# Adaptive units of a down step emitted in two parts, and the gathering matmul of a finished vector three units later

## The chip, the core and the metric

One core of one Trainium2 chip runs the program. The metric is the device time of one execution in microseconds; the time before is the median of three runs. TensorE (PE in the profile; its weight loads are PEld) multiplies matrices into PSUM, VectorE (DVE) and ScalarE (ACT) work element by element, GpSimd (POOL) does a little, and SyncE (SP) issues most of the loads. Each engine runs its own queue of instructions in order and waits on semaphores of the others.

## The reference: what is computed

Two trunk layers over 512 latent tokens of width 1024. Layer 0 mixes with neighbourhood attention and HGRN2 heads (with 256 context tokens), layer 1 with a short gated convolution; each layer ends in a gated feed-forward part of width 2816. Six adaptive vectors per layer (shift, scale and gate of both halves) come from the conditioning vector `c`:

```
mod = silu_c @ ada_w[layer] + ada_b[layer]
shift_m, scale_m, gate_m, shift_f, scale_f, gate_f = jnp.split(mod, 6, axis=-1)
...
x = x + gate_m[:, None, :] * y
h = modulate(rms_norm(x, norm_ffn_w[layer]), shift_f, scale_f)
x = x + gate_f[:, None, :] * conv_ffn(h, ffn_w_up[layer], ffn_conv_w[layer],
                                      ffn_conv_b[layer], ffn_w_down[layer])
...
def conv_ffn(h, w_up, conv_w, conv_b, w_down):
    a, val = jnp.split(h @ w_up, 2, axis=-1)
    return (jax.nn.gelu(dwconv3(a, conv_w, conv_b), approximate=False) * val) @ w_down
```

`ada_w` is 1024 by 6144 for each layer, 25 MB, and is used for one row vector only.

## The kernel before

Activations lie transposed: channels on the 128 partitions, tokens along the free dimension. Each matrix product is made of three matmuls (`mm3`, L287 to L290): weights and activations are split into a high and a low half, and high×high, high×low and low×high are added in PSUM. `Weights` loads raw weights with SyncE into two buffers `wraw` (1 MB a load as a rule), makes the high half `whi` with a copy on ScalarE (L92) and the low half `wlo` with a subtraction on VectorE (L93); three buffers of each kind go round, so a copy waits until TensorE has left the oldest.

**The adaptive vectors** that are not needed at once are made on VectorE in the background by `Ada`, in 160 units. A unit loads a slice `ar` of `ada_w` (128 by 512, 256 KB; three buffers, loaded by SyncE two units ahead, L485) and adds slice times conditioning into the accumulator `aa` (L502 for the first of eight slices, L504 for the others). After eight units a transposing reduction (L508) gives `ad`; this ends one half of a vector. A later unit, counted in calls, issues `gather`, a matmul on TensorE of `ad` with a selecting matrix into the PSUM tile `pad` (L514), and a still later one `finish`, four small additions on VectorE into `mod` (L520) and for the scales one more (L524). 20 such halves are made, the first of layer 0's mixer aside.

**Where units are issued.** 54 units are woven into layer 0's mixer. Then `units(n)` issues them in blocks: four in layer 0's output projection, five in each of eleven steps of layer 0's down projection, three at a time in layer 1's convolution mixer, four in each of two steps of its output projection, and two after groups of its feed-forward up part.

**The steps of the down projection** are in `project_back`. It makes 256 output channels at a time (four pairs `m`) and for each pair three groups of 6, 8 and 8 of the 22 input blocks. A step takes two weight tiles, then issues five units, then the matmuls of the first output tile `o[0]` (8 blocks by 3 matmuls of 512 columns is 24), then those of `o[1]`. The order of the built program need not be the order of the code: a scheduler places each instruction in its engine's queue by its own estimate of when its inputs are there, except where `pin` holds the order of the code.

Of the kernel before, what the change touches and what calls it, by code (L numbers as in the profile page):

```python
# [174 lines left out]
def backbone(ctx: ExitStack, tc: tile.TileContext, a, out, dump=None):  # L175
# [107 lines left out]
    def split(hi, lo, src):  # L283
        S.copy(hi, src)
        V.tensor_tensor(lo, src, hi.bitcast(F32), ALU.subtract)

    def mm3(o, wh, wl, mh, ml, start, stop):  # L287
        TE.matmul(o, wh, mh, start=start, stop=False, skip_group_check=True)  # L288
        TE.matmul(o, wh, ml, start=False, stop=False, skip_group_check=True)  # L289
        TE.matmul(o, wl, mh, start=False, stop=stop, skip_group_check=True)  # L290
# [183 lines left out]
    class Ada:  # L474
# [3 lines left out]
        n, calls, raw, late = 0, 0, {}, []  # L478
# [9 lines left out]
        def unit(self, aux):  # L488
            self.calls += 1
            while self.late and self.late[0][0] <= self.calls:  # L490
                self.late.pop(0)[1]()
            if self.n >= 8 * len(self.jobs):
                return
            r = self.n % 8
            l, p_, j = self.jobs[self.n // 8]
            while len(self.raw) < min(self.n + 3, 8 * len(self.jobs)):
                self.load()
            raw = self.raw[self.n]
            self.n += 1
            if r == 0:  # L500
                self.acc = ap_.tile([P, T], F32, tag="aacc", name=f"aa{self.n}", bufs=1)
                pin(V.tensor_scalar(self.acc[:], raw[:], sil[:, 0, 0:1], None, ALU.mult))  # L502
                return
            pin(V.scalar_tensor_tensor(self.acc[:], raw[:], sil[:, r, 0:1], self.acc[:], ALU.mult, ALU.add))  # L504
            if r < 7:
                return
            red = ap_.tile([P, 16], F32, tag="ared", name=f"ad{self.n}", bufs=1)
            V.tensor_reduce(red[:], self.acc[:].rearrange("p (b j) -> p b j", j=32), axis=AX.X, op=ALU.add,  # L508
                            apply_transpose=True)
            pm = []  # L510

            def gather():
                pm.append(aux(f"pad{l}{p_}{j}"))
                TE.matmul(pm[0][:, 0:16], sel, red[:], start=True, stop=True)  # L514

            def finish():
                c = p_ * 8 + 4 * j
                for qd in range(4):
                    s4 = slice(32 * qd, 32 * qd + 32)
                    V.tensor_tensor(mod[s4, l, c : c + 4], pm[0][s4, qd:16:4], abT[s4, l * 48 + c : l * 48 + c + 4],  # L520
                                    ALU.add)
                if p_ in (1, 4):
                    w0 = (16 if p_ == 1 else 32) + 8 * l + 4 * j
                    V.scalar_tensor_tensor(amul[:, 2 * l + (1 if p_ == 1 else 2), 4 * j : 4 * j + 4], mod[:, l, c : c + 4],  # L524
                                           1.0, pv[:, w0 : w0 + 4], ALU.add, ALU.mult)

            self.late += [(self.calls + 3, gather), (self.calls + 5, finish)]

    ada = Ada()

# [450 lines left out]
    def mms(o, w, src, base, k0, k1, c, first, last):  # L981
        wh, wl = w
        for k in range(k0, k1):
            hh, hl = src[k]
            mm3(o[:, c], wh[:, k - base], wl[:, k - base], hh[:, c], hl[:, c], first and k == base, last and k == k1 - 1)
# [49 lines left out]
    def project_back(nm, src, groups, gate, norm, start=0):  # L1035


        A, B = HALF
        steps = [(m, g_) for m in range(start, 4) for g_ in range(len(groups))]

        for n, (mp_, gi) in enumerate(steps):
            k0, k1 = groups[gi]
            if gi == 0:
                o = [acc_t(f"pb{nm}{mp_}{i}") for i in range(2)]
            w = [ws.get(), ws.get()]
            first, lastg = gi == 0, gi == len(groups) - 1
            if n == len(steps) - 1:
                break
            if n == len(steps) - 2:
                ws.spare = [(gq, f"q{2 * i}", f"q{2 * i + 1}") for i in range(3)]  # L1050
                ws.ahead(4)
            if n < len(steps) - 2 or len(groups) > 1:
                units(4 if len(groups) == 1 else 5)
            for i in range(2):
                mms(o[i], w[i], src, k0, k0, k1, slice(0, T), first, lastg)
                if lastg:
                    norm.back(o[i], 2 * mp_ + i, slice(0, T), gate)
                    if mp_ or i:
                        norm.add(slice(0, T))

        cut = (k0 + 3 * k1) // 4
        ws.ahead(4)
        mms(o[0], w[0], src, k0, k0, k1, A, first, True)
        norm.back(o[0], 6, A, gate)
        norm.add(A)
        log_exp_table()
        mms(o[1], w[1], src, k0, k0, k1, A, first, True)
        norm.back(o[1], 7, A, gate)
        norm.add(A)
        mms(o[0], w[0], src, k0, k0, cut, B, False, False)  # L1070
        norm.total(A)
        norm.scale(A)
        mms(o[0], w[0], src, k0, cut, k1, B, False, True)
        mms(o[1], w[1], src, k0, k0, k1, B, False, True)
        norm.back(o[0], 6, B, gate)
        oa = norm.outs(A)
        for _ in range(4):
            next(oa)
        norm.add(B)
        norm.back(o[1], 7, B, gate)  # L1080
        next(oa)
        next(oa)
        norm.add(B)
        for _ in oa:
            pass

        def rest():
            norm.total(B)
            norm.scale(B)
            for _ in norm.outs(B):  # L1090
                pass

        return rest

    def pair(nm, src):

        w = [ws.get(), ws.get()]
        o = [acc_t(f"pp{nm}{i}") for i in range(2)]
        for i in range(2):
            mms(o[i], w[i], src, 0, 0, KT, slice(0, T), True, True)  # L1100
        return o

    def quad(nm, src, rest, done=lambda: None):

        w = [ws.get(0) for _ in range(4)]
        o = [acc_t(f"pp{nm}{i}") for i in range(4)]
        for c in HALF:
            for k in range(KT):
                for i in range(4):
                    hh, hl = src[k]  # L1110
                    mm3(o[i][:, c], w[i][0][:, k], w[i][1][:, k], hh[:, c], hl[:, c], k == 0 and c.start == 0,
                        k == KT - 1)
                if c.start == 0 and k == 3:
                    rest()
        done()
        ws.pin = pin
        ws.ahead(2)
        ws.pin = lambda i: i
        return o[:2], o[2:]
# [91 lines left out]
    def conv3(t, src, w0, w1, w2, b):  # L1211
        S.activation(t[:], src, AF.Identity, scale=w1, bias=b)
        V.scalar_tensor_tensor(t[:, 1:], src[:, : T - 1], w0, t[:, 1:], ALU.mult, ALU.add)
        V.scalar_tensor_tensor(t[:, : T - 1], src[:, 1:], w2, t[:, : T - 1], ALU.mult, ALU.add)
# [8 lines left out]
    def units(n):  # L1223
        for _ in range(n):
            ada.unit(aux_t)
# [52 lines left out]
    for j in range(4):  # L1278
        if j == 0:
            oc, ou = quad("c", nrm.h, rest)  # L1280
        else:
            oc = pair(f"c{j}", nrm.h)
            units(3)
        cs = []
        for i in range(2):
            t = gp.tile([P, T], F32, tag=f"g{16 + i}", name=f"cs{j}{i}")
            S.copy(t[:], oc[i][:])
            cs.append(t)
        if j:
            ou = pair(f"u{j}", nrm.h)  # L1290
            units(3)
        ts_ = []
        for i in range(2):
            m = 2 * j + i
            V.tensor_tensor(cs[i][:], ou[i][:], cs[i][:], ALU.mult)
            t = fp.tile([P, T], F32, tag="t", name=f"sc{m}", bufs=5)
            conv3(t, cs[i], rowv(76 + m, 1), rowv(84 + m, 1), rowv(92 + m, 1), rowv(68 + m, 1))
            ts_.append(t)
        ob = pair(f"b{j}", nrm.h)
        units(3)  # L1300
        for i in range(2):
            m = 2 * j + i
            mh = gp.tile([P, T], F32R, tag=f"g{2 * m}", name=f"mch{m}")
            ml = gp.tile([P, T], F32R, tag=f"g{2 * m + 1}", name=f"mcl{m}")
            V.tensor_tensor(ob[i][:], ob[i][:], ts_[i][:], ALU.mult)
            split(mh[:], ml[:], ob[i][:])
            mix.append((mh, ml))
# [120 lines left out]
```

## Time and profile before

| | |
|---|---|
| median of 3 runs (lowest, highest) | 1335.97 us (1333.49, 1336.93) |
| the profiled execution's own time | 1333.99 us |
| its span in the trace | 1332.2 us |
| busy: TensorE, VectorE, ScalarE | 1304.5, 965.4, 625.2 us |
| mean granted clock of TensorE | 0.995 |

The span is the stretch from the first to the last instruction; the time holds 1.8 us more around it. A matmul's end is modelled, and matmuls overlap, so spacing is read from the starts. An engine's idle time is put down to what released it. Times in the trace count from the span's start.

### The profile page before, as it was taken

What the parts mean: (1) busy time and instruction counts of PE and PEld (TensorE: products, weight loads), DVE (VectorE), ACT (ScalarE), POOL (GpSimd) and SP (SyncE); (2) the same over time, 40 slices, a digit from 0 to 9 for tenths busy, and PEclk for the clock granted to TensorE, in tenths of its full rate; (3) what the DMA queues carried; (4) which work ended last, traced back from release to release, by engine and by line L of the source; (5) the groups of instructions that cost most, each with busy time, mean ns of one, the idle gap of its engine ahead of it and who ended that gap; (6) DMA issues with size and microseconds to landing.
All of it is one profiled execution on the core that took longest, in us unless ns stands there. A gap on an engine that the chain in (4) does not pass through costs nothing. (4 is left out here: it accounts for less than half of the span.)

```text
span 1332.2 us, 21229 instructions
## 1 busy us (share of the span) xinstructions
PE 1304.5 (98%) x8456; PEld 1147.6 (86%) x8456; DVE 965.4 (72%) x1688; ACT 625.2 (47%) x1085; POOL 84.3 (6%) x87
## 2 busy tenths in 40 slices
PE   7999999999999999999999999999999999999997
PEld 4798888888779998889877898888999989899997
DVE  4668897887778878788766776667789897782333
ACT  4443445555545656565422253223456565663223
POOL 2204332311000000000000000000000000000000
PEclk9999999999999999999999999999999999999999
DMA  9842113674562122323466734555403423242231
GB/s 293 265 123 84 33 33 82 152 182 134 153 206 96 64 99 92 127 71 119 141 211 198 226 132 143 167 165 174 158 27 117 142 80 127 80 146 69 91 108 64
DMA packets 134995, 172.35 MB, mean 129 GB/s; under 512 B 14320, under 2 KB 103792, under 8 KB 129776
## 3 DMA queue, kind: packets, MB, share of 16 engines
q1 hardware_dynamic: 132896, 166.15, 39.3%
q10 hardware_dynamic: 2000, 4.85, 1.4%
q8 instruction: 66, 1.08, 0.3%
q14 instruction: 33, 0.27, 0.1%
HBM read 165.21 MB, written 2.10 MB: 126 GB/s over the span
## 5 line engine op out<-in xcount | busy, mean ns | idle before, releaser
L92 ACT CAST whi<-wraw 128x1024 fp32r<-128x1024 f32 (+1 forms) x122 | 124.1, 1021 | 280.8 <-PE pd L1340 70.4
L93 DVE TENSOR_TENSOR wlo<-wraw,whi 128x1024 fp32r<-128x1024 f32 (+1 forms) x122 | 145.2, 1192 | 107.7 <-ACT whi L92 107.1
L288 PE MATMUL p<-hf,whi 128*128 128x512 f32 (+1 forms) x640 | 215.4, 338 | 1.4 <-ACT whi L125 1.4
L290 PE MATMUL p<-hf,wlo 128*128 128x512 f32 (+1 forms) x640 | 214.6, 335 | 0.0
L289 PE MATMUL p<-hf,whi 128*128 128x512 f32 (+1 forms) x640 | 214.1, 335 | 0.0
L125 ACT CAST whi<-wraw 128x512 fp32r<-128x512 f32 (+1 forms) x160 | 113.0, 727 | 85.0 <-PE p L289 35.0
L290 PEld LDWEIGHTS p<-hf,wlo 128*128 128x128 f32 x640 | 120.1, 188 | 13.6
L288 PEld LDWEIGHTS p<-hf,whi 128*128 128x128 f32 x640 | 120.1, 188 | 12.3 <-ACT whi L125 1.6
L289 PEld LDWEIGHTS p<-hf,whi 128*128 128x128 f32 x640 | 120.1, 188 | 10.7
L126 DVE TENSOR_TENSOR wlo<-wraw,whi 128x512 fp32r<-128x512 f32 (+1 forms) x160 | 128.1, 817 | 0.9 <-ACT whi L125 0.5
L504 DVE SCALAR_TENSOR_TENSOR aa<-ar,sil,aa 128x512 f32<-128x512 f32 x140 | 104.8, 749 | 24.1 <-DMA ar<-in_ada_w_dram 21.8
L1339 PE MATMUL pd<-whi,g 128*128 128x256 f32 x352 | 98.2, 279 | 0.0
L1341 PE MATMUL pd<-wlo,g 128*128 128x256 f32 x352 | 98.1, 279 | 0.0
L1340 PE MATMUL pd<-whi,g 128*128 128x256 f32 x352 | 97.9, 278 | 0.0
L288 PE MATMUL pbd<-g,whi 128*128 128x512 f32 (+1 forms) x192 | 73.5, 383 | 0.0
L289 PE MATMUL pbd<-g,whi 128*128 128x512 f32 (+1 forms) x192 | 73.3, 382 | 0.0
L290 PE MATMUL pbd<-g,wlo 128*128 128x512 f32 (+1 forms) x192 | 73.1, 381 | 0.0
L288 PE MATMUL p<-T,whi 128*128 128x256 f32 x240 | 69.0, 288 | 0.0
L290 PE MATMUL p<-T,wlo 128*128 128x256 f32 x240 | 67.2, 280 | 0.0
L289 PE MATMUL p<-T,whi 128*128 128x256 f32 x240 | 67.2, 280 | 0.0
L1340 PEld LDWEIGHTS pd<-whi,g 128*128 128x128 f32 x352 | 66.3, 188 | 0.0
L1339 PEld LDWEIGHTS pd<-whi,g 128*128 128x128 f32 x352 | 66.1, 188 | 0.0
(679 smaller groups left out, 3296.3 us busy)
## 6 DMA issues: line engine op xcount, KB each, us to landing
ar<-in_ada_w_dram SPq DMA_DIRECT2D x160, 256.0 KB, 3.1
wraw<-in_upq_dram SPq DMA_DIRECT2D x40, 1024.0 KB, 4.8
wraw<-in_ffn_w_down_dram SPq DMA_DIRECT2D x16, 1024.0 KB, 5.3
wraw<-in_od_w_in_dram SPq DMA_DIRECT2D x12, 1024.0 KB, 5.6
wraw<-in_ev_w_in_dram SPq DMA_DIRECT2D x20, 512.0 KB, 5.2
araw<-in_ada_w_dram SPq DMA_DIRECT2D x16, 512.0 KB, 6.3
wraw<-in_ffn_w_down_dram SPq DMA_DIRECT2D x8, 768.0 KB, 4.7
wraw<-in_ev_w_out_dram SPq DMA_DIRECT2D x4, 1024.0 KB, 6.9
```

The lines of the kernel that those rows point to most:

```text
L92: self.nc.scalar.copy(hv, rv)
L93: self.pin(self.nc.vector.tensor_tensor(lv, rv, hv.bitcast(F32), ALU.subtract))
L125: self.nc.scalar.copy(hi, src)
L126: V.tensor_tensor(lo, src, hi.bitcast(F32), ALU.subtract)
L288: TE.matmul(o, wh, mh, start=start, stop=False, skip_group_check=True)
L289: TE.matmul(o, wh, ml, start=False, stop=False, skip_group_check=True)
L290: TE.matmul(o, wl, mh, start=False, stop=stop, skip_group_check=True)
L504: pin(V.scalar_tensor_tensor(self.acc[:], raw[:], sil[:, r, 0:1], self.acc[:], ALU.mult, ALU.add))
L1339: TE.matmul(o[i][:, 0:256], gh[:, ts], w[0][:, k - k0], start=k == 0, stop=False)
L1340: TE.matmul(o[i][:, 0:256], gl[:, ts], w[0][:, k - k0], start=False, stop=False)
L1341: TE.matmul(o[i][:, 0:256], gh[:, ts], w[1][:, k - k0], start=False, stop=k == FT - 1)
```

## The change

Two numbers and two places are changed. The gather of a finished vector half is issued six calls after its last unit instead of three, and its finish eight instead of five. In `project_back` the units of a step are issued in two parts: two ahead of the first output tile's matmuls, and the rest (three in the down steps, two in the steps with one group) between the two tiles. The third block of each convolution step issues four units instead of three. The units, loads, reductions, gathers and finishes are the same in number; lines behind the second place move by two.

```diff
-            self.late += [(self.calls + 3, gather), (self.calls + 5, finish)]
+            self.late += [(self.calls + 6, gather), (self.calls + 8, finish)]
...
             if n < len(steps) - 2 or len(groups) > 1:
-                units(4 if len(groups) == 1 else 5)
+                units(2)
             for i in range(2):
                 mms(o[i], w[i], src, k0, k0, k1, slice(0, T), first, lastg)
+                if i == 0 and (n < len(steps) - 2 or len(groups) > 1):
+                    units(2 if len(groups) == 1 else 3)
                 if lastg:
                     norm.back(o[i], 2 * mp_ + i, slice(0, T), gate)
...
         ob = pair(f"b{j}", nrm.h)
-        units(3)
+        units(4)
```

The first piece is TensorE's queue in the second step of the down projection, before: `pbd000` and `pbd001` are the step's two output tiles, `whi` and `wlo` the halves of their weights, `g` the activations, and `pad051` the gather of the half `ad64`. First the last matmuls of the first tile, and then:

```order
L288 MATMUL pbd000_6919<-g0130_6051,whi130_6867 128x512
L289 MATMUL pbd000_6919<-g0131_6052,whi130_6867 128x512
L290 MATMUL pbd000_6919<-g0130_6051,wlo130_6868 128x512
L514 MATMUL pad051_7000<-ad64_6991,cst_70 128x16
L288 MATMUL pbd001_6920<-g060_5347,whi131_6978 128x512
L289 MATMUL pbd001_6920<-g061_5348,whi131_6978 128x512
```

In the changed program the same gather stands behind the second tile's 24 matmuls, ahead of the third step's first:

```order
L288 MATMUL pbd001_6920<-g0130_6051,whi131_6974 128x512
L289 MATMUL pbd001_6920<-g0131_6052,whi131_6974 128x512
L290 MATMUL pbd001_6920<-g0130_6051,wlo131_6975 128x512
L514 MATMUL pad051_7067<-ad64_6991,cst_70 128x16
L288 MATMUL pbd000_6919<-g0140_6199,whi132_6980 128x512
L289 MATMUL pbd000_6919<-g0141_6200,whi132_6980 128x512
```

It has moved by 24 matmuls. The gather `pad101` of the half `ad80` moves likewise, from row 3754 of TensorE's queue, where 20 matmuls of the fifth step stand ahead of it, to row 3806, behind the first tile of the sixth step: by 52. The last of the six, of `ad104`, moves from row 3984 to row 4001.

The second piece is VectorE's queue from the reduction of that first half on, before: `wlo_7057` is a low half of weights, and the row with `pad` the four additions that finish the vector.

```order
L508 TENSOR_REDUCE ad_6991<-aa_4176 128x16
L502 TENSOR_SCALAR aa_6995<-ar_6939,sil 128x512
L520 TENSOR_TENSOR mod<-pad_7000,vec 32x4 x4
L93 TENSOR_TENSOR wlo_7057<-wraw_6865,whi_7056 128x1024
L504 SCALAR_TENSOR_TENSOR aa_6995<-ar_6988,sil,aa_6995 128x512
```

And in the changed program:

```order
L508 TENSOR_REDUCE ad_6991<-aa_4200 128x16
L502 TENSOR_SCALAR aa_6995<-ar_6953,sil 128x512
L93 TENSOR_TENSOR wlo_7055<-wraw_6865,whi_7054 128x1024
L504 SCALAR_TENSOR_TENSOR aa_6995<-ar_6988,sil,aa_6995 128x512
L504 SCALAR_TENSOR_TENSOR aa_6995<-ar_6993,sil,aa_6995 128x512
L504 SCALAR_TENSOR_TENSOR aa_6995<-ar_7021,sil,aa_6995 128x512
L520 TENSOR_TENSOR mod<-pad_7067,vec 32x4 x4
```

The four additions have moved behind one subtraction and three multiply-adds.

## Rows read from the trace of the kernel before

**Rows 1.** The page: span, TensorE's busy time, and VectorE's multiply-adds of the units.
```profile
span 1332.2 us, 21229 instructions
...
PE 1304.5 (98%) x8456; PEld 1147.6 (86%) x8456; DVE 965.4 (72%) x1688; ACT 625.2 (47%) x1085; POOL 84.3 (6%) x87
...
L504 DVE SCALAR_TENSOR_TENSOR aa<-ar,sil,aa 128x512 f32<-128x512 f32 x140 | 104.8, 749 | 24.1 <-DMA ar<-in_ada_w_dram 21.8
```

**Rows 2.** Waits of TensorE, longest first: total us, times, longest.
```profile
PE prx L412 <- ACT sqx L410: 5.1, 1, 5.1
PE pad L514 <- DVE ad L508: 3.7, 2, 1.9
PE pkc L626 <- DVE sc L609: 2.2, 2, 1.5
```

**Rows 3.** Windows of 10 us: length, busy times, PEclk granted, DMA share, GB/s.
```profile
10.00:20.00 10.00, 7.29 (x40) 3.78 (x42) 5.81 (x20) 4.04 (x7) 2.13 (x2) 0.86 1.17 317
...
120.00:130.00 10.00, 8.45 (x57) 7.32 (x56) 10.00 (x18) 3.77 (x8) 5.09 (x5) 1.00 0.14 33
...
660.00:670.00 10.00, 8.09 (x35) 6.33 (x34) 6.22 (x12) 2.10 (x2) 0.00 (x0) 0.95 0.67 213
670.00:680.00 10.00, 10.00 (x41) 8.06 (x40) 5.68 (x8) 0.83 (x1) 0.00 (x0) 0.88 0.68 222
...
700.00:710.00 10.00, 8.18 (x31) 6.45 (x30) 5.22 (x10) 1.04 (x1) 0.00 (x0) 0.83 0.64 195
```

**Rows 4.** Timeline of TensorE, first wait: start, us, instruction, idle before.
```profile
663.18 0.39 PE L289 MATMUL pbd<-g,whi 128*128 128x512 f32 x1
...
666.16 0.39 PE L290 MATMUL pbd<-g,wlo 128*128 128x512 f32 x1
668.45 0.40 PE L514 MATMUL pad<-ad,cst 128*128 128x16 f32 x2 [1.91 <-DVE ad L508]
668.70 0.48 PE L288 MATMUL pbd<-g,whi 128*128 128x512 f32 x1
...
672.66 0.39 PE L289 MATMUL pbd<-g,whi 128*128 128x512 f32 x1
```

**Rows 5.** Timeline of TensorE, second wait.
```profile
699.86 0.40 PE L289 MATMUL pbd<-g,whi 128*128 128x512 f32 x1
702.07 0.36 PE L514 MATMUL pad<-ad,cst 128*128 128x16 f32 x2 [1.82 <-DVE ad L508]
702.28 0.48 PE L290 MATMUL pbd<-g,wlo 128*128 128x512 f32 x1
...
706.71 0.39 PE L290 MATMUL pbd<-g,wlo 128*128 128x512 f32 x1
```

**Rows 6.** Timeline of VectorE, ahead of both waits.
```profile
666.11 1.54 DVE L504 SCALAR_TENSOR_TENSOR aa<-ar,sil,aa 128x512 f32<-128x512 f32 x2 [2.94 <-DMA ar<-in_ada_w_dram]
667.69 0.71 DVE L508 TRANSPOSE_TENSOR_REDUCE ad<-aa 128x16 f32<-128x512 f32 x1
...
700.42 0.75 DVE L504 SCALAR_TENSOR_TENSOR aa<-ar,sil,aa 128x512 f32<-128x512 f32 x1 [1.93 <-DMA ar<-in_ada_w_dram]
701.21 0.71 DVE L508 TRANSPOSE_TENSOR_REDUCE ad<-aa 128x16 f32<-128x512 f32 x1
```

**Rows 7.** Timeline of SyncE's issues ahead of the first wait.
```profile
659.11 0.37 SPq L63 DMA_DIRECT2D wraw<-in_ffn_w_down_dram  x1
659.77 9.51 SPq L485 DMA_DIRECT2D ar<-in_ada_w_dram  x6
```

**Rows 8.** Timelines: a low half made, and the matmuls that use it.
```profile
688.25 1.23 DVE L93 TENSOR_TENSOR wlo<-wraw,whi 128x1024 fp32r<-128x1024 f32 x1 [0.38 <-ACT whi L92]
...
695.51 0.39 PE L288 MATMUL pbd<-g,whi 128*128 128x512 f32 x1
```

**Rows 9.** Timelines: the last low half for the convolution stage, and its first matmul.
```profile
773.95 1.22 DVE L93 TENSOR_TENSOR wlo<-wraw,whi 128x1024 fp32r<-128x1024 f32 x1
...
783.63 0.28 PE L288 MATMUL ppc<-hm,whi 128*128 128x256 f32 x1
```

## The prediction

> **What bounds the kernel now.** I read the page first: TensorE's matmuls are busy for 1304.5 of 1332.2 us [rows 1], so nothing off TensorE can win or lose time unless TensorE waits for it. The list of what TensorE waited for comes next [rows 2]. Its longest entry, 5.1 us, is at the start, and the next is the gathering matmul `pad` waiting for the reduction `ad`: 3.7 us in two waits, the longer 1.9. That is the matmul this change moves. The third is 2.2 us, in the first layer's HGRN part, at most 1.5 us at a time.
>
> The windows of 10 us put the two waits at 660 to 670 and 700 to 710 [rows 3], both in layer 0's down projection, and show something the list does not: the granted clock is under 1.00 in 660:670, 670:680 and 700:710. In the timeline of TensorE [rows 4] matmuls of 512 columns start every 0.229 us up to the wait ((666.16 − 663.18) / 13). The gather then starts at 668.45, where 666.39 was its turn. Behind it ten matmuls take from 668.70 to 672.66, so 0.40 us each. The second wait reads the same [rows 5]: the turn was 700.09, the gather started at 702.07, and the twelve matmuls from 702.28 end at 706.71.
>
> Why the reduction is late stands in VectorE's timeline [rows 6]. Before both waits VectorE stands idle for a slice `ar` of the adaptive weights, 2.94 and 1.93 us; the reduction starts at 667.69 and 701.21 and takes 0.71 us, so it ends at 668.40 and 701.92, 0.05 and 0.15 us ahead of the gather. The slices come late because SyncE issues them behind a load of 1 MB: `wraw` at 659.11, the slices from 659.77 [rows 7].
>
> **The change part by part.**
>
> *The gather three units later.* In the new order the first of these gathers stands 24 matmuls further on (the first piece of order above), so its turn comes at 666.39 + 24 × 0.229 = 671.89 us, 3.5 us after the reduction's end. The second stands 52 matmuls later, 11.9 us, where 1.8 would do. What is removed is 668.45 − 666.39 = 2.06 us and 702.07 − 700.09 = 1.98 us, together 4.04 us. The gather itself, two matmuls of 16 columns, stays.
>
> *The clock behind the waits.* Ten matmuls in 3.96 us instead of 2.29, and twelve in 4.43 instead of 2.75: 1.67 + 1.68 = 3.35 us. I count this as given back, since each slow stretch follows its wait directly, and the only other window shown with a lower clock, 10:20, lies around the 5.1 us wait at the start; the waits of up to 1.5 us at 120 to 130 left the clock at 1.00 [rows 2, 3]. The windows agree in size: the clock has two levels, 2.4 and 1.2 GHz, and the share not granted is (0.05 + 0.12) × 10 = 1.7 us behind the first wait and 0.17 × 10 = 1.7 us behind the second.
>
> The Trainium skill's page "TensorE: Matmul & The Clock Gate", section "Why this matters for your kernels", blames a drop in the middle of a kernel on idle gaps longer than either of these two waits. By that rule they would not be the cause, and only the 4.04 us would come back. The trace speaks against it here, and I weigh it as the second rival below.
>
> *The units in two parts.* Five units per step remain five: the same multiply-adds (749 ns each [rows 1]), reductions and loads of `ar`, 55 in layer 0's down steps. Three of the five now stand behind the first tile's matmuls in the program, so TensorE's own work lies between them and the first two. Four of the seven reductions of this stage move back by that as well, but their gathers move further. The shortest way from the start of a unit group that ends a vector to its gather is 36 matmuls in the new order (8.2 us), the longest 72. The worst lateness in the trace is the first wait's: TensorE began that step 24 matmuls ahead of 666.39, at 660.89, and the reduction ended 7.5 us later. So every gather clears it, the tightest by 0.7 us, at a place where before 19 matmuls sufficed. Cost: none on TensorE.
>
> What could be delayed on VectorE is the subtraction that makes the low half of the next weights, which queues behind the units. The cover is its lead: a half made by 688.25 + 1.23 = 689.48 was first used in the matmul group that starts at 695.51 [rows 8], 6 us, the shortest lead that I found in this stage. At the stage's end the last half for the next layer is done at 773.95 + 1.22 = 775.17 and its matmuls start at 783.63 [rows 9], 8.5 us. TensorE comes there 7.4 us earlier now, but these subtractions wait on buffers that TensorE releases, so they come earlier with it; without that cover the price would be nothing down to 1.1 us of lead, and then each microsecond one for one.
>
> *Four units in the convolution stage instead of three.* Four more units there in all, and as many fewer in the last layer: 4 × 0.75 = 3 us of VectorE and four loads of 256 KB in a stretch of 150 us in which TensorE waited for nothing in its list. Their cost is 0, hidden behind the same leads.
>
> *The first layer, where the scheduler reorders.* Six gathers stand in the first layer's mixer and move too, and with them some transposes, matmuls of projections and many small VectorE rows change places. The trace prices none of this. Bounds: a gain of at most 2.2 us, the largest wait of that part [rows 2], and a loss of as much, one more wait of that size. I take 0: none of these gathers waited before, and the moved pieces are the same work.
>
> Sum: 4.04 + 3.35 = 7.4 us off the profiled execution's 1333.99 us gives 1326.6. That execution lies 2 us under the median shown (1335.97) and 1.5 under the mean of the three runs, 1335.5; from that mean the forecast is 1328 us, or −0.55%. About 0.3%, 4 us, is what a measurement of this kernel can tell from no change: its three runs span 3.4 us.
>
> **The rivals.**
>
> *The wait moves instead of going.* VectorE still stands idle for slices behind each 1 MB load, and a reduction now in the second part of a step is held for the first tile's time too. If one or two of the gathers from the down steps on are still late by some 2 us, each costs up to 2.0 + 1.7 us as before, and the time is 1331 to 1335.5. Against it: the margins above, 0.7 to 10 us. Chance 0.13.
>
> *The clock stretches stay.* If what lowers the clock at 668 and 703 is not the wait but the steady load, the stretches would come back somewhere: only 4.04 us are gained, 1331.4 us. Against it: of the windows of 10 us between 20 us and 1320 us no other lies under 0.97. Chance 0.07 (this is what the page's rule comes to).
>
> *VectorE held at the gather.* Slower than before: the four additions that finish a vector wait, in VectorE's own queue, for a gather that now stands later in TensorE's. What queues behind them is the subtraction for the next weights. If VectorE is held there for more than the 6 us lead, TensorE waits for the low half at a half step's start. One such stall with its slow stretch costs about 3.7 us, and it takes three beyond the 7.4 us gained to pass 1339.5. It decides only from 6 us on. Against it: in the new order the first vector's additions stand behind one more subtraction and three multiply-adds (second piece of order), so VectorE comes to them later as well. Chance 0.05.
>
> **How the numbers follow.** Both waits gone and the clock kept: 0.75, its own range 1325.5 to 1330.5 (the 2.2 us of the first layer on either side, and where a median may fall). The range to report reaches into the first two rivals: 1324.5 to 1333, which leaves out the worse part of the moving wait, the slower case, and tails, together under 0.2. Faster by over 0.3%: 0.75 + half of 0.07 + a little of 0.13, 0.80. Within 0.3%: 0.14. Slower: 0.06.
>
> **What would show it.** In the new profile TensorE's list holds no `pad` entry, or one far under 1 us; the granted clock is 1.00 in every window from 20 us to the last; all six gathers of the down steps start some microseconds behind the end of their reductions, while VectorE still idles 2 to 3 us for `ar` at the same loads; the convolution stage starts near 776 us. I am wrong if a window's clock below 0.95 shows without a wait before it, if `pad` or a low half `wlo` appears in TensorE's list, or if the stages ahead of layer 0's down projection take over 2 us more or less.

## The result and the profile after

The changed kernel takes 1339.32 us (median of 20 executions, 1336.29 to 1343.50), the kernel before 1335.22 beside it (20 executions): a ratio of 1.0034, with a 95% interval of 1.0026 to 1.0043, so 4.5 us slower (3.5 to 5.7). The medians differ by 4.1 us; the ratio is taken over all executions, and the differences in time below go by ratios. Forecast were 1328 us and a gain.

The page, TensorE's list of waits and the windows of 10 us of the changed kernel (columns as in [rows 2, 3]):

```profile
span 1335.1 us, 21226 instructions
...
PE 1306.0 (98%) x8456; PEld 1148.9 (86%) x8456; DVE 966.7 (72%) x1688; ACT 624.5 (47%) x1085; POOL 83.2 (6%) x87
```

```profile
PE prx L412 <- ACT sqx L410: 5.8, 2, 5.2
PE pbo L288 <- DVE xT L1002: 5.0, 1, 5.0
PE pkc L626 <- DVE sc L609: 2.4, 2, 1.5
...
PE pbd L288 <- DVE xT L1002: 0.7, 1, 0.7
```

```profile
410.00:420.00 10.00, 5.02 (x34) 4.81 (x33) 6.84 (x11) 4.33 (x6) 0.00 (x0) 0.83 0.47 174
420.00:430.00 10.00, 10.00 (x71) 9.79 (x71) 6.42 (x16) 5.29 (x12) 0.00 (x0) 0.83 0.07 29
660.00:670.00 10.00, 10.00 (x45) 8.06 (x44) 8.53 (x12) 4.93 (x7) 0.00 (x0) 1.00 0.39 117
670.00:680.00 10.00, 10.00 (x47) 8.19 (x45) 6.47 (x8) 1.12 (x2) 0.00 (x0) 1.00 0.66 210
700.00:710.00 10.00, 10.00 (x44) 8.09 (x43) 6.56 (x11) 1.92 (x2) 0.00 (x0) 1.00 0.66 211
```

What the change aimed at has happened: `pad` is gone from TensorE's list, and the windows that stood at 0.95, 0.88 and 0.83 [rows 3] stand at 1.00. But a new entry of 5.0 us stands second, with two windows at 0.83 around it, at 412 us, in layer 0's output projection, far ahead of the down projection. Read by the first start of each kind of tile, the profiled execution goes:

| first start of | before | after | shift |
|---|---|---|---|
| `pbo` (output projection) | 362.96 | 363.82 | +0.86 |
| `pnf` (norm behind it) | 414.25 | 421.64 | +7.38 |
| `pbd` (down projection) | 652.46 | 660.54 | +8.08 |
| `pbd` of 256 columns (its last step) | 771.98 | 772.86 | +0.88 |
| `ppc` (convolution stage) | 783.63 | 786.21 | +2.58 |
| end of the span | 1332.18 | 1335.10 | +2.92 |

So 8.1 us were lost ahead of the down projection, 7.2 won in it, 1.7 lost again in its last step, and 0.3 behind that. Of the 8.1 us, 0.9 stand at `pbo` already; order_only below, whose queues are those of the kernel before up to there, starts `pbo` 1.1 us late as well, so this part can be scatter between executions. This execution took 1336.89 us, 2.4 under its median; a second profile of the same kernel (below) shows +4.2 us, as the times do.

The timeline of TensorE shows the new wait:

```profile
411.31 0.28 PE L290 MATMUL pbo<-mgh,wlo 128*128 128x256 f32 x1
...
412.37 0.28 PE L290 MATMUL pbo<-mgh,wlo 128*128 128x256 f32 x1
417.63 0.58 PE L288 MATMUL pbo<-mnh,whi 128*128 128x256 f32 x1 [4.98 <-DVE xT L1002]
418.01 0.41 PE L289 MATMUL pbo<-mnl,whi 128*128 128x256 f32 x1
...
421.64 1.05 PE L1014 MATMUL pnf<-sqaf,ones 128*128 128x256 f32 x2
```

Matmuls of 256 columns started every 0.118 us, so the next one's turn was 412.49: 5.1 us of waiting. The 18 up to 421.64 then take 4.0 us instead of 2.1. It is the pattern of [rows 4] again, in another place: a wait, and a stretch at the lower of the two clock levels behind it.

Why is `xT` late? Followed back, it leads over VectorE to a load, and from the load to a buffer. The timelines of SyncE's issues, first of before and then of after:

```profile
386.08 0.38 SPq L63 DMA_DIRECT2D wraw<-in_ev_w_out_dram  x1
386.50 3.75 SPq L485 DMA_DIRECT2D ar<-in_ada_w_dram  x3
392.05 0.38 SPq L63 DMA_DIRECT2D wraw<-in_ffn_w_up_dram  x1
394.70 2.13 SPq L485 DMA_DIRECT2D ar<-in_ada_w_dram  x2
400.35 0.38 SPq L63 DMA_DIRECT2D wraw<-in_ffn_w_up_dram  x1
403.22 7.69 SPq L63 DMA_DIRECT2D wraw<-in_upq_dram  x2
```

```profile
386.91 0.38 SPq L63 DMA_DIRECT2D wraw<-in_ev_w_out_dram  x1
387.34 10.68 SPq L485 DMA_DIRECT2D ar<-in_ada_w_dram  x5
399.61 2.77 SPq L63 DMA_DIRECT2D wraw<-in_ffn_w_up_dram  x2
408.39 8.55 SPq L63 DMA_DIRECT2D wraw<-in_upq_dram  x2
```

The first load of the next stage's weights goes out 7.6 us later, behind five slices instead of three, and the one of `upq` 5.2 us later. A weight load needs one of the two `wraw` buffers, which is free when both its blocks have been split into halves. The timelines of ScalarE, before and after, tell when that was:

```profile
389.72 1.05 ACT L92 CAST whi<-wraw 128x1024 fp32r<-128x1024 f32 x1 [2.34 <-PE pbo L289]
393.51 1.05 ACT L92 CAST whi<-wraw 128x1024 fp32r<-128x1024 f32 x1 [2.74 <-DMA wraw<-in_ev_w_out_dram]
```

```profile
394.70 2.00 ACT L92 CAST whi<-wraw 128x1024 fp32r<-128x1024 f32 x2 [7.66 <-DMA wraw<-in_ev_w_out_dram]
```

Before, ScalarE copied block 31 (the second half of a buffer that had landed long ago) at 389.72 and then waited for block 33 of the load still on its way. In the changed program the two have changed places in ScalarE's queue: the order before is

```
L92 CAST whi31_4239<-wraw15_3908 128x1024
L92 CAST whi33_4249<-wraw16_4160 128x1024
```

and after it is `whi33`, `whi31`. So ScalarE waits 7.66 us for the load, and block 31, which before was copied at 389.72, stands behind it. The Trainium skill's page "PSUM — Partial Sum Buffer", section "Engine vs sequencer instructions", calls the queues of ScalarE and VectorE strictly first in, first out; the trace agrees: 7.66 us idle with a landed block next in line. VectorE's queue has turned in the same sense:

```profile
395.38 0.48 DVE L502 TENSOR_SCALAR aa<-ar,sil 128x512 f32<-128x512 f32 x1 [3.68 <-DMA ar<-in_ada_w_dram]
395.79 1.22 DVE L93 TENSOR_TENSOR wlo<-wraw,whi 128x1024 fp32r<-128x1024 f32 x1
...
398.37 1.21 DVE L93 TENSOR_TENSOR wlo<-wraw,whi 128x1024 fp32r<-128x1024 f32 x1
...
413.37 0.69 DVE L108 TENSOR_TENSOR ws<-wraw 128x512 f32<-128x512 f32 x1 [1.48 <-DMA wraw<-in_upq_dram]
...
417.10 0.47 DVE L1002 SCALAR_TENSOR_TENSOR xT<-pbo,mod,xT 128x256 f32<-128x256 f32 x1
```

The low half of block 31 is the one at 398.37; it ends at 399.58, and the load goes out at 399.61. Before, it stood ahead of the unit that waits for a slice and ended at 392.02. From there the delay runs through the loads to the `xT` at 417.10 for which TensorE waits; before it was made at 411.08.

What turned these queues? Of half 48, the last that ends in the mixer, the gather is now issued with the last woven unit and the additions fall among the output projection's units (before, both lay in the mixer). The units of this step are also split. Which of the two does it, and whether by the order, had to be shown.

### The profile page after: what moved, and what is told of

It reads as the page before. It is cut to its first block, busy times and chain, and to the rows that moved or that the text cites. A ratio compares the mean times of both kernels' runs of the same rounds, so it can differ in the third digit from the quotient of the medians.

```text
span 1335.1 us, 21226 instructions
## 1 busy us (share of the span) xinstructions
PE 1306.0 (98%) x8456; PEld 1148.9 (86%) x8456; DVE 966.7 (72%) x1688; ACT 624.5 (47%) x1085; POOL 83.2 (6%) x87
## 5 line engine op out<-in xcount | busy, mean ns | idle before, releaser
L92 ACT CAST whi<-wraw 128x1024 fp32r<-128x1024 f32 (+1 forms) x122 | 123.8, 1021 | 267.9 <-PE pd L1342 70.4
L290 PEld LDWEIGHTS p<-hf,wlo 128*128 128x128 f32 x640 | 120.1, 188 | 13.7
L288 PEld LDWEIGHTS p<-hf,whi 128*128 128x128 f32 x640 | 120.1, 188 | 12.1 <-ACT whi L125 1.4
L289 PEld LDWEIGHTS p<-hf,whi 128*128 128x128 f32 x640 | 120.2, 188 | 10.7
L126 DVE TENSOR_TENSOR wlo<-wraw,whi 128x512 fp32r<-128x512 f32 (+1 forms) x160 | 127.9, 817 | 0.7 <-ACT whi L125 0.2
```

The lines of the kernel that those rows point to most:

```text
L92: self.nc.scalar.copy(hv, rv)
```

## The experiments

A summary first; times in us, read from the starts in each run's one profile. "Matmuls" is the time from the first `pbd` to its first matmul of 256 columns, "stage" the time on to the first `ppc`, "last reduction" its end, counted from the first `pbd`, "end wait" TensorE's wait for `xT` in the last step, "load" the issue of the first `ffn_w_up` weights, "o0 wait" TensorE's wait for `xT` near 412 us.

| run | matmuls | stage | last reduction | end wait | load | o0 wait | time to before (95%) |
|---|---|---|---|---|---|---|---|
| before | 119.5 | 131.2 | 121.1 | none | 392.1 | none | 1 |
| after | 112.3 | 125.7 | 118.3 | 0.7 | 399.6 | 5.0 | 1.0034 (1.0026, 1.0043) |
| after_again | 112.3 | 126.4 | 119.0 | 1.4 | 400.1 | 5.0 | one execution, 1338.20 us |
| late_down_split | 112.3 | 129.8 | 121.6 | 4.0 | 392.0 | none | 0.9972 (0.9962, 0.9982) |
| late_down_whole | 112.2 | 126.9 | 119.5 | 2.0 | 392.3 | 0.9 | 0.9960 (0.9945, 0.9975) |
| late_all_whole | 112.2 | 130.1 | 121.8 | 4.3 | 400.3 | 5.4 | 1.0017 (1.0006, 1.0027) |
| split_early | 120.1 | 131.9 | 122.4 | none | 393.1 | none | 0.9983 (0.9972, 0.9994) |
| order_only | 120.6 | 132.3 | 122.4 | none | 402.8 | 2.3 | 1.0035 (1.0023, 1.0047) |
| after_low_ahead | 112.3 | 126.4 | 119.1 | 1.5 | 399.1 | 4.8 | 1.0019 (1.0009, 1.0028) |
| after_order_back | 112.3 | 127.9 | 119.6 | 2.0 | 393.5 | 4.8 | 1.0038 (1.0025, 1.0052) |
| after_31_first | 112.3 | 127.2 | 119.9 | 2.3 | 393.8 | 2.1 | 0.9999 (0.9988, 1.0010) |
| after_31_first_b | 112.3 | 129.5 | 121.3 | 3.7 | 393.0 | 0.5 | 0.9994 (0.9986, 1.0003) |
| fewer_in_last | 112.2 | 123.8 | fewer units | none | 394.0 | 0.4 | 0.9946 (0.9934, 0.9958) |
| fewer_in_last_early | 120.2 | 131.9 | fewer units | none | 393.4 | none | 1.0012 (1.0000, 1.0024) |

### Which part of the change does what

**late_down_split**: the change, but the late gather only from the down step on.

```diff
-            self.late += [(self.calls + 6, gather), (self.calls + 8, finish)]
+            d = 3 if self.calls < 60 else 6
+            self.late += [(self.calls + d, gather), (self.calls + d + 2, finish)]
```

> The change with one exception: a vector that is finished in the first layer's weave is gathered three units later as in the kernel before, and only those of the down step on six later. Theory Order (the gather of half 48 and its adds, carried into the output projection's units, turned VectorE's and SyncE's order there): the 5.0 us wait of TensorE for `xT` at 412 us and the half clock behind it are gone, `pnf` starts within 1 us of 414.25, the down projection keeps its gain, and the time is 5 to 6 us under the kernel before (7.2 us saved between 652 and 772 us, 1.7 us lost at the end of the step). Rival Split (the units in two parts of the output projection step themselves hold up the weights): the wait at 412 us stays near 5 us and the time is within 2 to 5 us above the kernel before, as with the change.

The wait at 412 us is gone and `pnf` starts at 413.98: the split of the units is not what costs time there. The saving fell short, 3.7 us instead of 5 to 6, since the last step of the down projection gave back 5.9 us and not 1.7.

**late_down_whole**: the same late gather, and no split (the kernel before with these lines, and four units in the convolution stage).

> No step's units are split; the gather is six units later from the down step on, three units later in the first layer, and four units stand in the convolution stage. Theory Either (the late gather alone is enough, since the two gathers that waited now stand in the next step, two matmul groups behind their reductions): no `pad` among TensorE's waits, clock 1.00 in the windows from 660 to 710 us, no wait for `xT` at the end of the down projection, time 7 us under the kernel before (6 to 8). Rival Both (units in one part before the step's first matmuls still hold the reduction up): `pad` waits of 1 to 2 us stay, time 0 to 4 us under the kernel before.

`pad` is gone from TensorE's list without the split, and the matmuls take 112.2 us as in the change. "Either" was right on that, wrong on the end: 2.0 us of waiting for `xT` stand there, and the time is 5.3 us under instead of 7.

**late_all_whole**: the kernel before with 6 and 8 for 3 and 5 everywhere, and four units in the convolution stage.

> No step's units are split; the gather is six units later everywhere, as in the change. Theory Order: the wait for `xT` at 412 us of 5 us and the half clock behind it are there without any split, 8 us lost at `pnf`, 7 us won back in the down projection, time within 0 to 2 us above the kernel before. Rival Split: no wait at 412 us, time 6 to 8 us under the kernel before.

The wait at 412 us is there, 5.4 us, and `pnf` starts 7.5 us late, with no step split. The late gather in the mixer is what brings it, and with it ScalarE's order of after, where the wait for the load comes ahead of two copies:

```profile
395.37 2.00 ACT L92 CAST whi<-wraw 128x1024 fp32r<-128x1024 f32 x2 [8.31 <-DMA wraw<-in_ev_w_out_dram]
```

In late_down_split, late_down_whole and split_early ScalarE copies block 31 first, at 389.64, 389.75 and 390.71 us, and waits for the load behind it, 2.55, 3.94 and 2.90 us. So in these runs the turned order, the late weight load and the wait of 5 us come together or not at all. The time is 2.3 us above, a little over what was expected, for the 4.3 us at the end of the down projection.

**split_early**: the kernel before with the units in two parts and four in the convolution stage, gather as before.

> Units in two parts as in the change, the gather three units later as in the kernel before. Theory Order: nothing lost at 412 us. Theory Either: the group of matmuls between the two parts, some 5 us, covers the reduction, so that `pad` waits are under 0.3 us together, and 1.7 us are lost at the end of the step: time 5 to 6 us under the kernel before. Rival Split: 8 us lost at 412 us, time 2 to 5 us above. Rival Both: `pad` waits of 1 to 2 us stay, time 1 to 4 us under.

Nothing is lost at 412 us. "Either" fails and "Both" holds: TensorE's list has the waits as before,

```profile
PE pad L514 <- DVE ad L508: 3.9, 2, 1.9
```

because the first of these gathers still stands behind the step's first 24 matmuls: before the change the scheduler had put it there already, though the code has it ahead of them. The split moves units in the code and not this gather in the queue; the other one that waits, of `ad80`, moves by four matmuls. The time is 2.3 us under that of the kernel before; the profile (its execution, 1336.54 us, was the longest of twelve) shows no saving, so where these 2.3 us come from stays open.

### The order in the output projection

**order_only**: the kernel before, and in one step of this projection VectorE's splits of weights are kept in the order of the code, which puts them behind the units.

```diff
+            ws.pin = pin if nm == "o0" and n == 1 else (lambda i: i)
             w = [ws.get(), ws.get()]
```

> The kernel before, with nothing of the change: in the second step of the first layer's output projection VectorE's low parts of the weights are kept in the program's order, so that unit 57 and the next stand ahead of the low part that frees the weight buffer, as they do in the changed kernel, and all five slices stand ahead of the weight load on SyncE. Theory Order: the order alone brings the loss: TensorE waits some 5 us for `xT` near 412 us, half clock follows, `pnf` starts 6 to 9 us later than 414.25, the time is 5 to 9 us above the kernel before. Rival Adds (the gather and the small adds of half 48 themselves cost the time in that step): nothing moves, the time is within 2 us of the kernel before.

The load goes out at 402.8, `pnf` starts 6.2 us late (1.1 us of it were there at `pbo` already), and the down projection 5.5 us late, where the change lost 8.1: an order of the queues brings a loss of several microseconds without any gather moved. The wait of 5 us and the lower clock that were expected did not come. The list has waits of 2.3 and 0.3 us for `xT` and of 0.3 for a low half; the rest stands in no wait of the list. The time is 4.7 us above, just below the 5 to 9 us expected, and not all of that is this step's: both `pad` waits of the down projection are still there and come to 4.8 us instead of 3.7.

Four runs try to put the order back in the changed kernel. **after_low_ahead** has the third block of weights split ahead of the units in the code:

```diff
+            if nm == "o0" and n == 0:
+                ws.ahead(2)
             if n < len(steps) - 2 or len(groups) > 1:
                 units(2)
```

> The changed kernel whole, with one call more: the third block of weights of the output projection is split before the step's first two units instead of behind them. Theory Order: the first weight load of the next stage is issued near 392 us instead of 399.6, the wait for `xT` at 412 us is under 1 us, `pnf` starts within 2 us of 414.25, the time is 2 to 5 us under the kernel before, as in the run with the late gather from the down step on and split units. Rival Adds: the wait stays 4 us or more, the time is 3 to 5 us above.

The load still went out at 399.08 and the wait stayed at 4.8 us, as the rival had it. It does not decide, because the edit did not do what it was for: ScalarE's queue still held block 33 ahead of block 31 (8.16 us idle there), and VectorE stood 6.66 us for the copy. **after_order_back** kept the splits of nine blocks in the order of the code as well:

```diff
-        self.nc.scalar.copy(hv, rv)
-        self.pin(self.nc.vector.tensor_tensor(lv, rv, hv.bitcast(F32), ALU.subtract))
+        own = self.own if 28 < self.nsub < 38 else (lambda i: i)
+        own(self.nc.scalar.copy(hv, rv))
+        own(self.nc.vector.tensor_tensor(lv, rv, hv.bitcast(F32), ALU.subtract))
...
-    pin = tc.keep_in_program_order
+    pin = ws.own = tc.keep_in_program_order
...
+            if nm == "o0" and n == 0:
+                ws.ahead(2)
             if n < len(steps) - 2 or len(groups) > 1:
                 units(2)
```

> The changed kernel whole, with the third block of weights split ahead of the step's units as in the run before, and with the splits of blocks 29 to 37 kept in the program's order on ScalarE and VectorE both, so that ScalarE no longer stands at the block that is still on its way while the one that has landed waits behind it. Theory Order: the first weight load of the next stage is issued at 391 to 394 us instead of 399, the wait for `xT` near 412 us is under 1.5 us, `pnf` starts within 2.5 us of 414.25 and the time is 1 to 5 us under the kernel before. Rival Adds (gather and adds of half 48 in that step cost it, whatever the order): wait of 4 us or more, time 3 us above.

Now the first load goes out at 393.47 as expected, but the second at 409.48: with so many blocks held, four splits stand behind the second step's `xT` in one row, and the second buffer comes free late. The wait is 4.8 us again. It is another miss of the edit, and it shows that all loads in the row have to be early, not the first alone. **after_31_first** and **after_31_first_b** hold as little as will do: block 31 is split between the two parts of the units, and on ScalarE blocks 31 to 33 (in the second run 31 and 33) keep the order of the code. The second run's edit:

```diff
-        self.nc.scalar.copy(hv, rv)
-        self.pin(self.nc.vector.tensor_tensor(lv, rv, hv.bitcast(F32), ALU.subtract))
+        hi_ = self.nc.scalar.copy(hv, rv)
+        if self.nsub in (31, 33):
+            self.own(hi_)
+        lo_ = self.pin(self.nc.vector.tensor_tensor(lv, rv, hv.bitcast(F32), ALU.subtract))
+        if self.nsub in (31,):
+            self.own(lo_)
...
-    pin = tc.keep_in_program_order
+    pin = ws.own = tc.keep_in_program_order
...
                 units(2)
+            if nm == "o0" and n == 0:
+                ws.ahead(2)
             for i in range(2):
```

> The changed kernel whole, with the third block of weights (31) split behind the step's first two units, and on ScalarE the blocks 31, 32 and 33 in the program's order, 31 kept in its place on VectorE too. SyncE's row of loads is then as in the kernel before, three slices ahead of the first weight load of the next stage, and on VectorE the first operation on the load behind it stands after the low halves' `xT`. Theory Order: that weight load is issued at 392 to 395 us and the next near 402, the wait for `xT` near 412 us is under 1.5 us, `pnf` starts within 2.5 us of 414.25, time 2 to 5 us under the kernel before. Rival Adds: the wait stays 4 us or more, time 3 us or more above.

> As the run beside it, but only blocks 31 and 33 are kept in order on ScalarE, and on VectorE the operation on the load of the `upq` weights stands ahead of the low halves' `xT`. Theory Order: if the loads are all issued some 7 us earlier than in the changed kernel, its place does no harm: wait near 412 us under 1.5 us, time 2 to 5 us under the kernel before. If only VectorE's place of that operation had mattered, the wait is 3 us or more here and under 1.5 us in the run beside it.

SyncE's issues of the second of the two:

```profile
387.42 4.00 SPq L489 DMA_DIRECT2D ar<-in_ada_w_dram  x3
392.95 0.38 SPq L63 DMA_DIRECT2D wraw<-in_ffn_w_up_dram  x1
396.20 1.26 SPq L489 DMA_DIRECT2D ar<-in_ada_w_dram  x2
402.24 0.38 SPq L63 DMA_DIRECT2D wraw<-in_ffn_w_up_dram  x1
405.12 7.45 SPq L63 DMA_DIRECT2D wraw<-in_upq_dram  x2
```

This is the row of before, 1 to 2 us later. The wait of 5.0 us is down to 0.5, `pnf` starts at 415.90 instead of 421.64, and the time falls from 4.5 us above the kernel before to its level (0.8 under, which is not clear of no change), with the gather and the additions of half 48 where the change put them. In the first of the two the second load goes out at 405.29, and 2.1 us of waiting remain, over the 1.5 expected. So the order of the queues is the cause, not the work in that step, and "Adds" is out. That the time is not 2 to 5 us under is again the end of the down projection (3.7 us of waiting).

### The end of the down projection

**after_again**: the changed kernel a second time.

> The changed kernel once more, for a second profile: the wait of 5 us at 412 us stands there again. If the end of the down projection hangs on when VectorE's last slices land, its wait for `xT` differs from the 0.7 us of the first profile, up to 4 us; if it hangs on the order alone, it is 0.7 us again.

The wait at 412 us is 5.0 us again, the one at the end 1.4 instead of 0.7. Over all runs with the late gather and five units a step it lies between 0.7 and 4.3 us, and the table shows why: the last reduction ends 118 to 122 us behind the start of the stage in all of them, as it did before (121.1), while TensorE now begins the last step after 112.3. The two go one for one: in each of the nine profiles the wait is the last reduction's end less 117.5 to 117.6 us (118.3 and 0.7 in after, 121.8 and 4.3 in late_all_whole). VectorE's waits between 640 and 800 us, before and after, say what it hangs on:

```profile
DVE aa L504 <- DMA ar<-in_ada_w_dram: 15.2, 12, 2.9
...
DVE xT L1002 <- PE pbd L290: 6.9, 5, 2.0
```

```profile
DVE aa L504 <- DMA ar<-in_ada_w_dram: 25.2, 14, 4.5
...
DVE xT L1002 <- PE pbd L290: 1.6, 1, 1.6
```

VectorE hardly waits for TensorE's tiles any more (1.6 us instead of 6.9); it waits for slices, 10 us longer. What makes the slices land at different times from run to run was not tried. And in the last step of after, `xT` stands right behind the last unit:

```profile
777.35 0.75 DVE L504 SCALAR_TENSOR_TENSOR aa<-ar,sil,aa 128x512 f32<-128x512 f32 x1 [1.41 <-DMA ar<-in_ada_w_dram]
778.13 0.71 DVE L508 TRANSPOSE_TENSOR_REDUCE ad<-aa 128x16 f32<-128x512 f32 x1
778.88 0.48 DVE L1002 SCALAR_TENSOR_TENSOR xT<-pbd,mod,xT 128x256 f32<-128x256 f32 x1
```

**fewer_in_last**: late_down_whole with one unit instead of five in the last down step that has any, and five instead of four in each of the four places of the convolution stage.

```diff
-                units(4 if len(groups) == 1 else 5)
+                units(4 if len(groups) == 1 else 5 if n < len(steps) - 2 else 1)
...
-        units(4)
+        units(5)
```

> The run with the late gather from the down step on and whole units, with four units fewer in the last down step that has any and one more in each of four places of the convolution stage. Theory Units (at the end of the down projection VectorE's last slices hold up `xT`, so that part of the 7.2 us is given back): no wait of TensorE for `xT` there, 2 us less in the trace up to the first `ppc`, time 7 to 9 us under the kernel before. Rival Weights (it is the loads of the next stage's weights that are late, with or without these units): a wait of 2 us or more stays, time 5 to 7 us under.

```profile
PE prx L412 <- ACT sqx L410: 5.9, 3, 5.3
PE pkc L627 <- DVE sc L610: 2.2, 2, 1.5
PE pq L288 <- ACT h L312: 1.4, 2, 1.2
```

Neither `pad` nor `xT` of the down projection is left in TensorE's list, of which these are the first rows. The stage takes 123.84 us instead of 131.17, 7.3 us less, and the time is 7.2 us under the kernel before (1327.87 us): the best of all, and the whole forecast saving. "Units" holds.

**fewer_in_last_early**: the same places and numbers of units (one, and five in the convolution stage instead of three), with the gather three units later as before.

> The kernel before with four units moved from the end of the down step to the convolution stage and nothing else: whole units, gather three units later everywhere. The late gather is what ends the two waits: here both `pad` waits stay, 1.5 to 2.5 us each with the half clock behind them, and the time is within 2 us of the kernel before. Rival (the moved units alone relieve VectorE and the queue, and so the reductions too): `pad` waits under 0.5 us together, time 6 to 8 us under, as with the late gather.

Both `pad` waits stay (1.5 and 3.5 us; 1.5 to 2.5 each were expected, and the lower clock follows the longer one only), and the time is that of the kernel before, or 1.6 us more. So the late gather is what ends the waits, and the relief at the end pays only with it.

## Why the prediction was wrong, step by step

**The two waits, 4.04 us, and the clock behind them, 3.35 us: right.** The sum of 7.4 us was measured as 7.2 (119.52 to 112.33 us), in every kernel with the late gather in the down steps. The clock came back with the waits, so the rival "the clock stretches stay" is out here, and with it what the Trainium skill's page "TensorE: Matmul & The Clock Gate", section "Why this matters for your kernels", would have made of it (4.04 us alone). One ground that I gave was misread: the 5.1 us wait at the start does not lie in the window 10:20, it ends at 5.07 us, and the changed kernel, with a wait of 5.2 us in the same place, has 10:20 at 1.00. TensorE's timeline of before, and the window of after:

```profile
5.07 6.54 PE L412 MATMUL prx<-sqx,ones 128*128 128x512 f32 x8 [5.07 <-ACT sqx L410]
```

```profile
10.00:20.00 10.00, 8.23 (x44) 3.79 (x47) 6.51 (x21) 4.29 (x8) 1.81 (x1) 1.00 1.17 316
```

**The margins: right.** The six gathers start 3.2 to 8.1 us behind their reductions; the first reads, from VectorE's and TensorE's timelines of after:

```profile
676.01 0.71 DVE L508 TRANSPOSE_TENSOR_REDUCE ad<-aa 128x16 f32<-128x512 f32 x1
...
679.96 0.29 PE L514 MATMUL pad<-ad,cst 128*128 128x16 f32 x2
```

VectorE still idles for `ar` in this stage, as foretold, though up to 4.5 us where 2 to 3 were named.

**Four units in the convolution stage, cost 0: nothing speaks against it.** TensorE's list has no wait of that stage for them, and from the first `ppc` to the end the two profiles of the changed kernel lose 0.3 and 1.0 us.

**"The first layer, where the scheduler reorders … I take 0", within 2.2 us either way: this step failed.** It cost 7 to 8 us (8.1 at the start of the down projection, 0.9 of them there at `pbo`): a wait of 5 us for `xT` in the output projection, behind a weight load that went out 7.6 us late because ScalarE's and VectorE's queues had landed work behind work whose load was on its way, and 2 to 3 us of lower clock. The bound was the largest wait that stood there before. That is no bound for a reordering: the waits of the new order are not in the old trace. And it was drawn around the mixer, where the gathers moved, while the loss arose in the step behind it, into which the last of them was pushed. The order of ScalarE's and SyncE's queues could be read beforehand; I read TensorE's and VectorE's in the down steps alone.

**"The units in two parts … Cost: none", covered by leads of 6 to 8.5 us at the low halves: this failed at the stage's end**, by 0.7 to 4.3 us. It is not the split that costs it: late_down_whole, without a split, waits 2.0 us there. The lead was read at the wrong row. The low halves do follow TensorE, as I argued, but the units follow their slices, and the `xT` that TensorE needs stands behind the last of them. Before, TensorE was late enough to hide that; 7.2 us saved used up the cover. The signs were in the trace: VectorE waiting 15.2 us for slices in this stage.

**The slower case** that I priced (VectorE held at the gather) is not what happened. VectorE's waits for `pad` did grow, none of them in the down steps; over the whole program, before and after:

```profile
DVE mod L520 <- PE pad L514: 2.9, 2, 1.7
```

```profile
DVE mod L520 <- PE pad L514: 9.3, 5, 3.5
```

but no wait of TensorE in the list names them. Whether those of the mixer have a part in the 0.9 us at `pbo` is not shown. The rival missing from my list was a weight load held up by the order of the queues.

**The sign that I named** did show it: the stages ahead of layer 0's down projection take 8 us more, where over 2 were to prove me wrong, and the convolution stage starts at 786.21 us instead of 776.

Open is why the scheduler's estimate sets block 33 ahead of block 31; it is in no trace.

## What to carry to other kernels

When a change moves background work in a program that a scheduler orders, read the new order of every queue over every stage that the moved instructions enter, ScalarE's copies and the loads too, and look for one rule broken: work whose input is there must not stand behind work whose input is on its way. Price such a place by what the queue behind it feeds (here one weight buffer freed 7.6 us late), not by the waits that the old trace shows.

When a wait is taken out of the engine that bounds a stage, ask when the other engines end that stage by their own inputs. The gain is whole only if they end earlier too; here four units moved out of the last step made the difference between 5.3 and 7.2 us.

## What the hardware showed that I had not expected

A wait's length alone did not tell whether the lower clock follows. Waits of TensorE of 1.8 to 2.8 us for `pad` were followed by matmuls at half speed ([rows 4, 5]; 1.95 and 1.90 us in split_early, 2.05 and 2.75 in order_only), and one of 1.50 us was not (fewer_in_last_early). Waits of 2.0 us (late_down_whole), 2.1 and 2.3 (after_31_first) and 2.3 (order_only) for `xT`, all in steps with matmuls of 256 columns, left the windows at 1.00, as the 2.1 us of after_31_first show:

```profile
410.00:420.00 10.00, 7.36 (x59) 6.90 (x58) 6.37 (x10) 5.38 (x8) 0.00 (x0) 1.00 0.54 196
420.00:430.00 10.00, 10.00 (x86) 9.95 (x85) 9.74 (x24) 6.67 (x15) 0.00 (x0) 1.00 0.00 0
```

But the wait of 2.0 us in after_order_back, for the same `xT` and at the same place as in late_down_whole, was followed by it:

```profile
780.00:790.00 10.00, 8.00 (x53) 7.62 (x52) 6.00 (x13) 5.45 (x10) 0.00 (x0) 0.83 0.53 184
```

So the width of the matmuls does not tell the cases apart either. All waits of 3.5 us and more in these two stages went with a window at 0.66 to 0.90. What sets the cases apart was not tried.
